# Alternating two heads' attention products between the halves of the matmul array

## The chip, the cores and the metric

The kernel runs on one core of a Trainium2 chip. The metric is the device time of one execution in microseconds (us). [...]

## The reference

The program is a small network of two blocks of two layers each. The change touches only the second block, where a layer is a mixer and a feed-forward part. Layer 0's mixer has, beside a gated part, neighbourhood attention with 8 heads of 64 over 256 tokens, whose keys are the 256 tokens (with a bias and a window) and 256 context tokens; the context stream attends to itself (256 keys). Layer 1's mixer has attention with 16 query heads of 64 and 4 heads of keys and values, over the same 512 keys. What is computed for a head, with q divided by the square root of 64:

```python
s = jnp.einsum('bqhgd,bkhd->bhgqk', qg, k).astype(jnp.float32) * (dh ** -0.5)
p = jax.nn.softmax(s, axis=-1).astype(v.dtype)
return jnp.einsum('bhgqk,bkhd->bqhgd', p, v)
```

## The kernel before

All of it is in float32. A product whose inputs were split into a high and a low part (`float32r`) is three matmuls that add up in PSUM (`mm3`, lines 355 to 357: high by high, high by low, low by high). A product of plain float32 is one matmul that shows as two records in the trace.

`attend_pair` does the attention of two heads whose q and k lie in partitions 0 to 63 and 64 to 127. It is called 16 times: in `even_mixer` for each of four chunks once for the context (`nk` = 256 keys) and once for the tokens (`nk` = 512, with a bias), in `odd_mixer` for each of eight chunks (`nk` = 512, with a scale). Before the change it goes head by head. For a head, and for each of two tiles `t` of 128 queries, it does

- the scores: three matmuls of 64 rows by 128 columns (lines 355 to 357) into a PSUM bank `sc`, of which there are two;
- `softmax`: the row maximum on DVE (line 1239, or 1236 with the bias added), its negative (1243, 1246), the exponential with the row sum on ACT (1244, 1247), the reciprocal and the scaling on DVE (1249, 1250);
- four (or two) transposes of the probabilities on PE (line 1268) into the one PSUM bank `pt`, and their copies to SBUF on ACT (line 1271) into tiles `pT`, of which there are four; a tile holds two blocks of 128 keys for both query tiles.

When a head's two tiles are done, the value products follow (line 1273): one matmul for each block `j` of 128 keys, 128 rows by 64 columns, into the head's half of the bank `po`. Then `split` (lines 1039, 1040) writes the result of both heads.

The instructions are not run in the order in which they are written: a scheduler orders each engine's queue ahead of time, instruction by instruction, from priorities that follow the written order, and from when it expects operands and buffers to be ready. So other matmuls, called fill below, stand between those of the attention: in `even_mixer` the projections of the next chunk and the gate (`project`, `gelu2`), in `odd_mixer` the projections of later queries (`query`) and the output projection (`out_products`). They are the matmuls into `acc`.

Of the kernel before, what the change touches and what calls it, by code (L numbers as in the profile page):

```python
# [13 lines left out]
PSUM = bass.MemoryType.PSUM  # L14
# [27 lines left out]
def block_list():  # L42
    """The weight blocks in the order in which they are used: (weight, layer, first chunk of 128 rows,
    number of chunks, first column, columns)."""
    out = []
# [98 lines left out]
def host_arrays(inp):  # L144
    """The inputs laid out for the chip, and constants that depend on shapes alone."""
    import numpy as np

    f = {k: np.asarray(v) for k, v in inp.items()}
    a = {}
# [130 lines left out]
class Net:  # L280
# [23 lines left out]

# [1 line left out]
    def con(self, pool, i):  # L306
# [11 lines left out]

# [1 line left out]
    def load(self):  # L320
# [16 lines left out]
    def weights(self, n=1):  # L337
        """The next n blocks: (hi, lo) by chunk of rows."""
        i = self.nuse
        self.nuse += n  # L340
        while self.nload < min(self.nuse + self.ahead, len(BLOCKS)):
            self.load()
        out = []
        for j in range(i, i + n):
            hi, lo = self.loaded.pop(j)
            out += [(hi[:, k], lo[:, k]) for k in range(BLOCKS[j][3])]
        return out
# [11 lines left out]
    def gemm(self, w, m, xs, cols, n, ps=None):  # L359
        """[128 columns m of the block, n tokens] in PSUM; xs: (hi, lo) by chunk."""  # L360
        if ps is None:
            ps = self.psum("acc")[:, :n]
        m = slice(128 * m, 128 * m + 128)
        for k, (wk, xk) in enumerate(zip(w, xs, strict=True)):
            self.mm3(ps, [t[:, m] for t in wk], [t[:, cols] for t in xk], k == 0, k == len(w) - 1)
        return ps

    def gemm_nat(self, w, xs, t, n, ps=None, m=0, first=True, last=True):
        """[128 tokens t, n columns of the block] in PSUM."""
        if ps is None:  # L370
            ps = self.psum("acc")[:, :n]
        m = slice(m, m + n)
        for k, (wk, xk) in enumerate(zip(w, xs, strict=True)):
            self.mm3(ps, [x[:, t] for x in xk], [x[:, m] for x in wk], first and k == 0, last and k == len(w) - 1)
        return ps

# [1 line left out]
    def rsqrt(self, src, shape, mul, add, name, pool=None):  # L378
        """1/sqrt(src * mul + add) on a small tile; RS^2 times its argument too if it goes to a pool of its own.
        A guess from the bits, a step of Newton with constants for the least error (under 7e-4), then one of third  # L380
        order (under 1e-9); the argument's factor RS^2 makes up for the factors that the steps leave out."""
        nc = self.nc
# [18 lines left out]
    def rsqrt1(self, a, b, name):  # L401
        """1/sqrt(a + b + 1024 eps), [128, 1], for columns RS^2 a and RS^2 b of sums over 1024 features, as rsqrt."""
        nc = self.nc
# [11 lines left out]
    def sumsq_add(self, ss, tmp_pool, src, first, n):  # L415
        """ss (+)= src^2, [128, n]."""
        nc = self.nc
# [7 lines left out]
    def rstd_row(self, pool, ss, tiles, width, mul, name, eps=EPS, extra=False):  # L425
        """[128, n] with 1/sqrt(mean + eps) of each token in each partition, from sums over chunks; and by
        token: the same and mean + eps, with a column for tokens 0 to 31 four times if extra."""
        nc = self.nc
# [19 lines left out]

# [1 line left out]
    def ada_prepare(self):  # L450
# [12 lines left out]
    def ada_steps(self):  # L463
        """Generator: the conditioning by groups of four units of 512 columns, each unit in rows of its own; a
        step is half of the columns for one chunk of the contraction."""
        nc = self.nc
# [42 lines left out]

# [1 line left out]
    def first_pre(self, c, g, sums=True):  # L511
        """The scaled, not yet normalized operand of chunk c of h, and its part of the sum of squares."""
        nc = self.nc
# [47 lines left out]
    def first_mixer(self, l, mp, fp):  # L561
# [17 lines left out]

        # queries and keys, not divided by the norm of h: its square joins eps in their own norms  # L580
        n_a = 42 if l == 0 else 40
# [39 lines left out]

        # recurrent branch: parameters
        bh = mp.tile([128, 8], F32, name="bh")
# [39 lines left out]

        # recurrent branch, and the first tile of queries
        xc, gts = [], []
# [62 lines left out]

        # output projection, recurrent half last
        oc = slice(0, T) if l + 1 < DEPTH else slice(META, T)  # L730
# [16 lines left out]
    def first_attend(self, mp, l, i, qk, vn, aq, nlam, sub, mh, ml):  # L747
        """Generator: the attention of a tile of queries, a step for each unit of heads and one for the rest."""
        nc = self.nc
# [81 lines left out]
    def gelu2(self, pool, out, x, n):  # L831
        """out = 2 * gelu(x), with the tanh form."""
        nc = self.nc
# [6 lines left out]
    def softplus(self, pool, L):  # L840
        """log(1 + exp(-L)) = max(-L, 0) + 2 atanh(z / (2 + z)), z = exp(-|L|), on [128, 4]."""
        nc = self.nc
# [30 lines left out]
    def first_ffn(self, l, gp, other):  # L873
        """other: steps of work that can be done in between."""
        nc = self.nc
# [51 lines left out]
    def ffn_whole(self, up):  # L927
        """Feed-forward of 256 tokens with the whole result in PSUM: [tile][half], natural."""
        y = [[self.psum("y") for _ in range(2)] for _ in range(2)]
# [25 lines left out]

# [1 line left out]
    def derive(self, l):  # L957
        """Gains of the norms before the branches, joined with the conditioning, times sqrt(1024)."""
        nc = self.nc
# [21 lines left out]
    def pair(self, n):  # L981
        """Room for both parts of a chunk of n tokens."""
        op = lambda: self.chunk(self.c2s, "op", OP_BUFS, F32R)
# [9 lines left out]
    def prepare_steps(self, l, i, s, xs, col, scratch, room, tag):  # L993
        """Generator: the operands of branch i (0: mixer, 1: feed-forward) for stream s, from column col on."""
        nc = self.nc
# [25 lines left out]
    def post(self, t, y, B, scratch, room):  # L1021
        """h += gate * gain * norm(y) for the tokens of tile t; y: two halves."""
        nc = self.nc
# [56 lines left out]
    def second_start(self):  # L1080
        """Room of the second block, and its second stream, which doesn't need the first block."""
        self.der = []
# [8 lines left out]
    def out_products(self, mp, y, half, mix, toks):  # L1091
        """One half of the products of the output projection; the second one on call, by tile of tokens."""
        nc = self.nc
# [135 lines left out]
    def softmax(self, pool, ps, nk, bias, scale):  # L1229
        """Rows of softmax(scale * ps + bias), [128, nk]; scale is None or a column."""  # L1230
        nc = self.nc
# [21 lines left out]
    def attend_pair(self, mp, heads, k0, nk, bias, scale, v, out):  # L1253
        """Two heads of 64: their results transposed, [128, 256], split into out.
        heads: (both parts of q of 256 tokens, of k, column of v) with q and k at rows 0 and 64."""
        nc = self.nc
        po = self.psum("po")[:, :256]
        for i, (q, k, vc) in enumerate(heads):
            r = slice(64 * i, 64 * i + 64)
            nj = nk // 128  # L1260
            pT = [self.chunk(mp, "pT", 4) for _ in range(nj // 2)]
            for t in range(2):
                ps = self.psum("sc")
                self.mm3(ps[:, :nk], [x[r, 128 * t:128 * t + 128] for x in q], [x[r, k0:k0 + nk] for x in k], True, True)
                p = self.softmax(mp, ps[:, :nk], nk, bias and bias(i, t), scale and scale(i, t))
                pt = self.psum("pt")
                for j in range(nj):
                    nc.tensor.transpose(pt[:, 128 * j:128 * j + 128], p[:, 128 * j:128 * j + 128], self.idt)  # L1268
                for jj in range(nj // 2):
                    dst = pT[jj].rearrange("p (j q) -> p j q", j=2)[:, :, 128 * t:128 * t + 128]  # L1270
                    nc.scalar.activation(dst, pt[:, 256 * jj:256 * jj + 256].rearrange("p (j q) -> p j q", j=2), AF.Copy)
            for j in range(nj):
                nc.tensor.matmul(po[r], v[k0 // 128 + j][:, vc:vc + 64], pT[j // 2][:, 256 * (j % 2):256 * (j % 2) + 256],  # L1273
                                 start=j == 0, stop=j == nj - 1, tile_position=(0, 64 * i))
        self.split(out, slice(0, 256), po)
# [196 lines left out]
```

## Time and profile before

| what | value |
|---|---|
| time, median of 3 runs | 1753.16 us (1750.38 to 1757.98) |
| span of the profiled execution | 1758.4 us |
| PE busy | 1700.8 us, 97% of the span |
| DVE, ACT busy | 1165.5 us (66%), 852.1 us (48%) |
| attention in the even mixer | about 799 to 914 us from the start of the span |
| attention in the odd mixer | about 1426 to 1542 us |

The span runs from the first to the last instruction of one profiled execution; no other time of that execution is shown. Busy time of an engine is the time in which at least one of its instructions runs.

### The profile page before, as it was taken

The numbers are of one execution on the slowest core, as the hardware profiler recorded it, in microseconds if no ns is written. First come the engines' busy times: TensorE is split into PE (matmuls) and PEld (weight loads), VectorE is DVE, ScalarE is ACT, GpSimd is POOL, SyncE is SP. The second block draws the span as 40 slices with busy tenths as digits, with TensorE's granted clock in tenths as the row PEclk, the third lists the DMA queues.
The fourth block names the chain that finished last, engine by engine and source line by source line (L and its number), as shares of the span: only waits on it lengthen the run. The fifth ranks groups of instructions, "written<-read, shape, count | busy, mean of one in ns | idle before, by whom it ended". The sixth has DMA issues, their size and how long they took to land.

```text
span 1758.4 us, 27995 instructions
## 1 busy us (share of the span) xinstructions
PE 1700.8 (97%) x10720; PEld 1419.9 (81%) x10720; DVE 1165.5 (66%) x2611; ACT 852.1 (48%) x1615; POOL 69.2 (4%) x142
## 2 busy tenths in 40 slices
PE   8999999999889999999999999999999899979998
PEld 7869999998559999996667777777888776569997
DVE  7678776676757766744557655464666866577777
ACT  5565444455636444534455543233233745565554
POOL 0000000000110000000100111010000000000000
PEclk9999999999999999999999999999999899989999
DMA  7446555553486666432223455464232321136663
GB/s 265 126 145 204 179 170 178 157 180 121 156 279 215 182 189 185 142 100 72 70 78 112 164 198 179 143 210 138 85 98 87 106 66 37 59 97 184 189 184 116
DMA packets 71797, 256.83 MB, mean 146 GB/s; under 512 B 8512, under 2 KB 8528, under 8 KB 71664
## 3 DMA queue, kind: packets, MB, share of 16 engines
q1 hardware_dynamic: 56624, 202.54, 37.7%
q0 software_dynamic: 14896, 52.51, 8.9%
q8 instruction: 84, 1.38, 0.3%
q14 instruction: 49, 0.40, 0.1%
q10 hardware_dynamic: 144, 0.00, 0.0%
HBM read 253.94 MB, written 1.08 MB: 145 GB/s over the span
## 4 chain that ended last, share of the span: by engine, by line
PE 86%; issue 6%; DVE 3%; DMA 3%; ACT 1%; POOL 0%; DVEq 0%; POOLq 0%; ACTq 0%
PE acc L355 16%; PE acc L356 16%; PE acc L357 15%; PE up L355 6%; PE up L356 6%; PE up L357 6%; PE po L1273 3%; DMA wada<-wada 3%; PE acc L476 2%; PE y L355 2%; PE y L357 2%; PE y L356 2%; PE pt L1268 2%; PE sc L355 1%; DVE wlo L333 1%
## 5 line engine op out<-in xcount | busy, mean ns | idle before, releaser
L332 ACT ACTIVATE whi<-raw 128x1024 fp32r<-128x1024 f32 (+2 forms) x436 | 397.0, 924 | 562.4 <-PE acc L356 254.1
L333 DVE TENSOR_TENSOR wlo<-raw,whi 128x1024 fp32r<-128x1024 f32 (+2 forms) x436 | 457.2, 1057 | 284.7 <-ACT whi L332 278.7
L355 PE MATMUL acc<-hi,whi 128*128 128x272 f32 (+1 forms) x848 | 248.0, 293 | 7.4 <-ACT hi L516 7.4
L357 PE MATMUL acc<-hi,wlo 128*128 128x272 f32 (+1 forms) x848 | 246.3, 290 | 0.8 <-DVE wlo L333 0.8
L356 PE MATMUL acc<-lo,whi 128*128 128x272 f32 (+1 forms) x848 | 246.9, 291 | 0.0
L355 PEld LDWEIGHTS acc<-hi,whi 128*128 128x128 f32 x848 | 161.6, 191 | 13.8 <-ACT hi L516 7.4
L356 PE MATMUL acc<-op,whi 128*128 128x256 f32 (+1 forms) x528 | 165.8, 315 | 0.2 <-DVE op L1018 0.2
L355 PE MATMUL acc<-op,whi 128*128 128x256 f32 (+1 forms) x528 | 164.7, 314 | 0.3 <-ACT qraw L1407 0.3
L357 PE MATMUL acc<-op,wlo 128*128 128x256 f32 (+1 forms) x528 | 164.1, 311 | 0.0
L356 PEld LDWEIGHTS acc<-lo,whi 128*128 128x128 f32 x848 | 161.6, 191 | 2.1 <-issue 0.4
L357 PEld LDWEIGHTS acc<-hi,wlo 128*128 128x128 f32 x848 | 161.9, 191 | 1.2 <-DVE wlo L333 0.8
L355 PE MATMUL acc<-whi,op 128*128 128x512 f32 (+1 forms) x432 | 154.9, 358 | 0.0
L356 PE MATMUL acc<-wlo,op 128*128 128x512 f32 (+1 forms) x432 | 154.1, 357 | 0.0
L355 PE MATMUL up<-op,whi 128*128 128x512 f32 (+1 forms) x384 | 147.0, 384 | 0.2 <-ACT pt L1016 0.2
L356 PE MATMUL up<-op,whi 128*128 128x512 f32 (+1 forms) x384 | 146.1, 381 | 0.0
L357 PE MATMUL up<-op,wlo 128*128 128x512 f32 (+1 forms) x384 | 145.4, 379 | 0.0
L355 PEld LDWEIGHTS acc<-op,whi 128*128 128x128 f32 x528 | 100.9, 192 | 10.0 <-issue 3.0
L356 PEld LDWEIGHTS acc<-op,whi 128*128 128x128 f32 x528 | 101.3, 192 | 8.9 <-issue 3.8
L357 PEld LDWEIGHTS acc<-op,wlo 128*128 128x128 f32 x528 | 101.4, 192 | 6.1 <-issue 1.9
L355 PEld LDWEIGHTS acc<-whi,op 128*128 128x128 f32 x432 | 81.2, 188 | 16.1 <-issue 4.6
L356 PEld LDWEIGHTS acc<-wlo,op 128*128 128x128 f32 x432 | 81.4, 188 | 15.0 <-issue 3.4
L355 PEld LDWEIGHTS up<-op,whi 128*128 128x128 f32 x384 | 73.0, 191 | 20.1 <-issue 5.4
(409 smaller groups left out, 3395.0 us busy)
## 6 DMA issues: line engine op xcount, KB each, us to landing
raw<-wts SPq DMA_DIRECT2D x362, 512.0 KB, 3.6
wada<-wada POOLq DMA_DIRECT2D x93, 512.0 KB, 4.7
raw<-wts SPq DMA_DIRECT2D x8, 384.0 KB, 3.1
B<-brow SPq DMA_DIRECT2D x6, 512.0 KB, 4.0
nb<-nbias POOLq DMA_DIRECT2D x16, 128.0 KB, 2.4
wada<-wada SPq DMA_DIRECT2D x3, 512.0 KB, 4.7
h<-xm SPq DMA_DIRECT2D x4, 272.0 KB, 5.0
gates<-gates SPq DMA_DIRECT2D x2, 512.0 KB
```

The costliest lines, as they stand in the source:

```text
L332: nc.scalar.activation(hi[:, cs], raw[:, cs], AF.Copy)
L333: nc.vector.tensor_tensor(lo[:, cs], raw[:, cs], hi[:, cs].bitcast(F32), op=ALU.subtract)
L355: mm(out, a[0], b[0], start=start, stop=False)
L356: mm(out, a[0], b[1], start=False, stop=False)
L357: mm(out, a[1], b[0], start=False, stop=stop)
L476: nc.tensor.matmul(ps[32 * j:32 * j + 32, 256 * half:256 * half + 256], self.cs[:, k], w[:, j], start=k == 0, stop=k + 1 == KD, tile_posit ...
L1268: nc.tensor.transpose(pt[:, 128 * j:128 * j + 128], p[:, 128 * j:128 * j + 128], self.idt)
L1273: nc.tensor.matmul(po[r], v[k0 // 128 + j][:, vc:vc + 64], pT[j // 2][:, 256 * (j % 2):256 * (j % 2) + 256], start=j == 0, stop=j == nj - ...
```

## The change

For one query tile the scores of both heads are now issued matmul by matmul in turn, head 0 in rows 0 to 63 of the array and head 1 in rows 64 to 127, each into a bank of its own. Then come the softmax, the transposes and the copies of head 0 and of head 1. When both query tiles of both heads are done, the value products are issued in turn, for each block of keys head 0 in columns 0 to 63 and head 1 in columns 64 to 127. The four `pT` tiles of a pair (two with 256 keys) are taken at once. The number of instructions, their shapes and the numbers of buffers are the same. Elsewhere the diff takes out comments alone.

```diff
     def attend_pair(self, mp, heads, k0, nk, bias, scale, v, out):
...
+        nc = self.nc
+        mm = nc.tensor.matmul
+        nj = nk // 128
+        rows = [slice(64 * i, 64 * i + 64) for i in range(2)]
         po = self.psum("po")[:, :256]
-        for i, (q, k, vc) in enumerate(heads):
-            r = slice(64 * i, 64 * i + 64)
-            nj = nk // 128
-            pT = [self.chunk(mp, "pT", 4) for _ in range(nj // 2)]
-            for t in range(2):
-                ps = self.psum("sc")
-                self.mm3(ps[:, :nk], [x[r, 128 * t:128 * t + 128] for x in q], [x[r, k0:k0 + nk] for x in k], True, True)
-                p = self.softmax(mp, ps[:, :nk], nk, bias and bias(i, t), scale and scale(i, t))
+        pT = [[self.chunk(mp, "pT", 4) for _ in range(nj // 2)] for _ in heads]
+        for t in range(2):
+            tok = slice(128 * t, 128 * t + 128)
+            ps = [self.psum("sc")[:, :nk] for _ in heads]
+            for n, (a, b) in enumerate(((0, 0), (0, 1), (1, 0))):
+                for i, (q, k, _) in enumerate(heads):
+                    mm(ps[i], q[a][rows[i], tok], k[b][rows[i], k0:k0 + nk], start=n == 0, stop=n == 2)
+            for i in range(2):
+                p = self.softmax(mp, ps[i], nk, bias and bias(i, t), scale and scale(i, t))
                 pt = self.psum("pt")
                 for j in range(nj):
                     nc.tensor.transpose(pt[:, 128 * j:128 * j + 128], p[:, 128 * j:128 * j + 128], self.idt)
                 for jj in range(nj // 2):
-                    dst = pT[jj].rearrange("p (j q) -> p j q", j=2)[:, :, 128 * t:128 * t + 128]
+                    dst = pT[i][jj].rearrange("p (j q) -> p j q", j=2)[:, :, tok]
                     nc.scalar.activation(dst, pt[:, 256 * jj:256 * jj + 256].rearrange("p (j q) -> p j q", j=2), AF.Copy)
-            for j in range(nj):
-                nc.tensor.matmul(po[r], v[k0 // 128 + j][:, vc:vc + 64], pT[j // 2][:, 256 * (j % 2):256 * (j % 2) + 256],
-                                 start=j == 0, stop=j == nj - 1, tile_position=(0, 64 * i))
+        for j in range(nj):
+            for i, (_, _, vc) in enumerate(heads):
+                mm(po[rows[i]], v[k0 // 128 + j][:, vc:vc + 64], pT[i][j // 2][:, 256 * (j % 2):256 * (j % 2) + 256],
+                   start=j == 0, stop=j == nj - 1, tile_position=(0, 64 * i))
         self.split(out, slice(0, 256), po)
```

## Rows read from the trace of the kernel before

**Rows 1.** The page: span, and the first line on engines.

```profile
span 1758.4 us, 27995 instructions
PE 1700.8 (97%) x10720; PEld 1419.9 (81%) x10720; DVE 1165.5 (66%) x2611; ACT 852.1 (48%) x1615; POOL 69.2 (4%) x142
```

**Rows 2.** Busy time by stretch: even attention, odd attention, what follows.

```profile
core 0: us, PE busy (x) PEld busy (x) DVE busy (x) ACT busy (x) POOL busy (x), PEclk, DMA share, GB/s
799.00:914.00 115.00, 115.00 (x509) 73.55 (x508) 63.56 (x182) 57.10 (x146) 11.88 (x30) 1.00 0.19 58
1426.00:1542.00 116.00, 116.00 (x553) 73.02 (x553) 69.08 (x210) 65.81 (x169) 0.00 (x0) 1.00 0.17 51
```

**Rows 3.** Waits, 1426 to 1542: who for whom, us, times, longest.

```profile
ACT pT L1271 <- PE pt L1268: 25.5, 29, 2.2
PEld po L1273 <- ACT pT L1271: 4.5, 13, 0.4
```

**Rows 4.** The same stretches, instructions on tile sc alone, then on po alone.

```profile
799.00:914.00 115.00, 23.90 (x96) 13.27 (x96) 17.57 (x32) 9.01 (x32) 1.00 0.19 58
1426.00:1542.00 116.00, 31.38 (x96) 14.95 (x96) 22.08 (x32) 27.62 (x64) 1.00 0.17 51
...
799.00:914.00 115.00, 25.00 (x96) 11.49 (x96) 3.40 (x8) 3.07 (x8) 1.00 0.19 58
1426.00:1542.00 116.00, 32.55 (x128) 15.63 (x128) 3.40 (x8) 3.07 (x8) 1.00 0.17 51
```

**Rows 5.** Timeline, PE: first block's scores, conditioning; start us, duration, line, form.

```profile
437.87 0.73 PE L766 MATMUL sc<-kr,qr 64*128 64x272 f32 x4
...
452.92 0.72 PE L766 MATMUL sc<-kr,qr 64*128 64x272 f32 x2
...
462.32 1.07 PE L476 MATMUL acc<-wada,cs 128*32 128x256 f32 x16
```

**Rows 6.** Timeline, PE: scores in the even and the odd mixer.

```profile
804.75 0.51 PE L355 MATMUL sc<-qkv 64*128 64x256 f32 x2
...
1434.02 0.49 PE L355 MATMUL sc<-y,qh 64*128 64x512 f32 x1
1434.44 1.94 PE L1273 MATMUL po<-pT,v 128*64 128x256 f32 x8
...
1436.89 0.50 PE L356 MATMUL sc<-y,qh 64*128 64x512 f32 x1
...
1524.12 0.49 PE L355 MATMUL sc<-y,qh 64*128 64x512 f32 x1
...
1525.71 0.50 PE L355 MATMUL acc<-whi,op 128*128 128x512 f32 x1
...
1528.02 0.50 PE L355 MATMUL sc<-y,qh 64*128 64x512 f32 x1
...
1528.91 0.50 PE L355 MATMUL acc<-whi,op 128*128 128x512 f32 x1
```

**Rows 7.** Timeline, PE: end of a pair in the odd mixer.

```profile
1516.62 0.66 PE L1268 MATMUL pt<-con,p 128*128 128x128 f32 x4
...
1518.09 0.66 PE L1268 MATMUL pt<-con,p 128*128 128x128 f32 x4
...
1519.38 1.08 PE L1273 MATMUL po<-pT,v 128*64 128x256 f32 x4
...
1520.82 1.08 PE L1273 MATMUL po<-pT,v 128*64 128x256 f32 x4
```

**Rows 8.** Groups by line and form, 1426 to 1542: count, busy us, mean ns.

```profile
L1247 ACT ACTIVATE p<-sc,snm,aq 128x512 f32<-128x512 f32 x32 | 24.9, 780 | 3.4 <-DVE snm L1246 3.3
...
L1271 ACT ACTIVATE pT<-pt 128x256 f32<-128x256 f32 x64 | 21.0, 380 | 25.5 <-PE pt L1268 25.5
...
L1250 DVE TENSOR_SCALAR p<-p,sr 128x512 f32<-128x512 f32 x32 | 15.5, 483 | 0.4
...
L1247 ACT ACTIVATION_READ_ACCUMULATOR p<-sc,snm,aq 128x1 f32 x32 | 6.5, 204 | 0.0
```

## The prediction

> **What bounds the kernel now.** I read the page first: PE is busy for 97% of the span, and a matmul's end is modelled there, so that alone doesn't say that PE sets the pace [rows 1]. The busy time by stretch comes next. In both stretches of attention PE is busy for all of 115 and of 116 us, while DVE has 55 to 60% and ACT 50 to 57%, at a granted clock of 1.00 [rows 2]. Then the waits decide who waits for whom: in the odd stretch ACT's copies stood idle 25.5 us for transposes from PE, while the weight loads of the value products waited only 4.5 us in total for ACT's copies, never over 0.4 us at a time [rows 3]. So in both stretches PE's queue is the bound, and the softmax runs ahead of it. Fill from other parts still stands between the attention's matmuls in the last pair of the odd stretch, at 1525.71 and 1528.91 [rows 6], so there is work that can move up. A microsecond taken off PE here is a microsecond off the end.
>
> How much is there to take? In the two stretches, instructions on the score banks keep PE busy for 23.9 and 31.4 us, those on the value bank for 25.0 and 32.6 us [rows 4]. Half of the 112.8 us, 56 us, is the ceiling for anything that lets two heads run side by side.
>
> **Can halves of the array run side by side?** The trace of before has it in other places. The first block's scores for two heads' halves of rows take 0.73 us as four records, and those of one half alone take 0.72 us as two records: the second half is free [rows 5]. For columns, the conditioning's products go to four groups of 32 columns: sixteen records of 256 columns take 1.07 us [rows 5], while four records of 256 columns in one head's half of `po` take 1.08 us [rows 7]. And even the scores of this very function do it by chance: two first matmuls together take 0.51 us, where one takes 0.50 (at 804.75, one of ten such places in the two stretches, each of a single matmul) [rows 6]. So I cost a matmul that goes beside one of the other half at nothing.
>
> **Prices.** Three score matmuls of 512 keys that stand alone take 0.89 us (1528.02 to 1528.91); six in a row take 1.59 us (1524.12 to 1525.71), so three more in the same run cost 0.70 us [rows 6]. For 256 keys I take half, an estimate. Value products: eight records, four products, take 1.94 us [rows 6], four records, two products, 1.08 us [rows 7]; a product costs 0.43 us.
>
> **If every product finds its partner.** There are 64 groups of three score matmuls, 48 of them with 512 keys: each stretch has 96 score matmuls [rows 4], 16 groups of the even one being narrow. The change makes 32 rounds of them, 24 wide and 8 narrow. A wide round saves 0.70 to 0.89 us, a narrow one half: 16.8 to 21.4 and 2.8 to 3.6 us. Of value products a wide pair has eight, a narrow one four, and half are hidden: 12 pairs at 4 x 0.43 = 1.72 us, or 1.94 where a whole run goes, and 4 at 0.86 to 1.08 us: 24.0 to 27.6 us. Together 44 to 53 us. That is one end.
>
> **What the order does to it.** The written order alternates, but the queue's order comes from readiness, instruction by instruction: the score group of 1434.02 is cut after its first matmul by eight value records and transposes, and its second comes at 1436.89 [rows 6]. In step with that, look at when partners become ready.
>
> Scores: head 0's bank is free when its exponential has run, head 1's one exponential later, 0.78 + 0.20 = 0.98 us [rows 8]. Head 0's three matmuls need 0.70 us. Unless PE is held up by something else, all three are gone before head 1 may start; they then pair with nothing. Both banks free at the same time is what a run of six, or one that begins to be one, shows. I find ten of those in the two stretches, the run at 1524.12 being one [rows 6], against 32 rounds. I take ten rounds that pair, four narrow and six wide: 4 x 0.35 + 6 x 0.70 = 5.6 us. Today's ten chance overlaps hide some 0.15 us each, and I let them go: 1.5 us. Net 4 us. The ends are -1.5 and 25 us.
>
> Value products: near the end of a pair two sets of transposes follow each other after 1.47 us, and the first product starts 1.29 us after the set that it needs [rows 7]. After the change these two sets are head 0's and head 1's of the second query tile. So head 0's first product starts before head 1's transposes; these (0.66 us) go next, and two copies of 0.38 us must follow [rows 8] before head 1 has its operands. Meanwhile head 0's second and third product run, and from there on both heads have products ready. Of eight, head 0's first stands alone, and the other seven take about five slots: six instead of eight. 2 x 0.43 us x 12 wide pairs = 10.3 us. In a narrow pair one of four: 0.43 x 4 = 1.7 us. Sum 12 us, ends 0 (head 0 always done first) and 27.6. The split into several runs costs nothing new: the last head of a pair is already split in two today, at 1519.38 and 1520.82 [rows 7].
>
> At 804.75 the two that run together stand next to each other in the queue [rows 6]. [...]
>
> **Other edits.** Softmax, transposes and copies keep their number and sizes; no DMA moves with them. The four `pT` go to one pair, so the first copy of the next pair waits for this pair's last value products, and behind it on ACT's queue stand exponentials and the casts of weights. I cost this at nothing: the next pair's transposes come behind these products anyway, and fill covers what is left. Its price without cover is the third rival.
>
> **Sum.** 4 + 12 = 16 us of PE. 1758.4 - 16 = 1742.4 us for an execution like the profiled one, whose span is 0.3% above the median; in the median's terms 1753.16 x 1742.4 / 1758.4 = 1737 us. With 16 us less PE work, ACT stands at 66 of some 108 us in the odd stretch, so it does not become the bound.
>
> **Rivals.**
> - All partners meet. If the scheduler's clock sees PE behind the softmax, as the chip does [rows 3], both heads' operands lie ready and the written order holds. 35 to 53 us: 1700 to 1718 us. Against it stands the cut group of 1434.02. Chance 0.15.
> - The alternation doesn't happen. Every first head is done before the second is ready; only the order of tiles changes. Then it gains or loses up to 9 us by what the scheduler puts elsewhere: 1744 to 1762 us. For it: 0.98 against 0.70 us. Chance 0.27.
> - Slower, by the `pT` tiles. If the next pair's first copies (0.76 us) and the exponential queued behind them (0.98 us) start only after the last value product, and no fill is ready, PE waits 1.7 us at each of 16 boundaries: 28 us, less the 16 us gained, 1765 us. It decides from 1 us of open wait at a boundary on. Against it: PE's fill between pairs, and PE now waits 0.4 us at most [rows 3]. Chance 0.08.
>
> The forecast, some partners meeting, has 0.50 and its own range 1718 to 1744 us. A measurement of this kernel can tell about 0.5%, 9 us, from no change. Faster: 0.15 + 0.50 = 0.65; same 0.27; slower 0.08. The range for 8 in 10 goes from 1712, in the first rival, to 1757, which leaves the slower rival and the top of the second out.
>
> **What would show it.** Right: both stretches shorter by 16 us together, by more in values than in scores; value records of both halves starting together in part, runs of sixteen records in some 3 us instead of two runs of eight at 1.94; most score groups still three matmuls of one head. Full alternation: score groups of six in 0.89 us throughout, and sixteen value records in 1.94. [...]

## The result and the profile after

| kernel | median | range of its runs |
|---|---|---|
| before | 1755.36 us | 1750.38 to 1757.98 (4 runs) |
| changed | 1726.58 us | 1726.08 to 1729.71 (4 runs) |

The ratio is 0.9839, with a 95% interval of 0.9819 to 0.9860: about 28 us faster (25 to 32). The forecast was 1737 us in a range of 1712 to 1757, faster with a chance of 0.65. The sign and the range held; the gain was 28 us where 16 were forecast.

The page of the changed kernel, span and first line on engines; [rows 1] are those of before. PE stands for TensorE's matmuls and PEld for its weight loads, listed apart; DVE is VectorE, ACT ScalarE, POOL GpSimd.

```profile
span 1725.0 us, 27991 instructions
...
PE 1669.8 (97%) x10720; PEld 1403.9 (81%) x10720; DVE 1163.6 (67%) x2611; ACT 851.0 (49%) x1615; POOL 69.8 (4%) x142
```

PE has the same number of records and 31 us less busy time, at the same share of a shorter span. DVE and ACT do what they did.

Busy time by stretch in the changed kernel, from the first score to the last value product of the even and of the odd attention. Columns as in [rows 2].

```profile
796.00:900.00 104.00, 103.59 (x505) 66.91 (x505) 62.15 (x181) 56.92 (x147) 12.14 (x28) 1.00 0.22 64
1412.00:1509.00 97.00, 96.97 (x546) 63.86 (x545) 67.95 (x208) 64.96 (x168) 0.00 (x0) 1.00 0.20 58
```

PE is still busy throughout at a granted clock of 1.00; ACT has risen to 67% of the odd stretch (64.96 of 97) and is not the bound. From the first score to the last value product the stretches were 113.0 and 113.9 us long in the profiled execution before (799.6 to 912.6, 1426.0 to 1539.9) and are 103.7 and 97.0 now (796.1 to 899.8, 1412.0 to 1508.9): 26.2 us less. The two spans differ by 33.4 us, more than the medians, because the profiled execution of before was one of the longer ones; the other 7 us are spread over the first 800 us (3.6), the time between the stretches (1.2) and the end (2.4).

Waits in the odd stretch of the changed kernel; [rows 3] are those of before.

```profile
ACT pT L1275 <- PE pt L1272: 15.3, 23, 1.2
...
PEld po L1278 <- ACT pT L1275: 3.5, 10, 0.4
```

Nothing has turned round: ACT's copies still wait for PE, and the weight loads of the value products wait 0.4 us at most for the copies.

Busy time with instructions on `po` alone, even and odd stretch of the changed kernel; [rows 4] are those of before.

```profile
790.00:915.00 125.00, 17.24 (x96) 7.60 (x96) 3.39 (x8) 3.04 (x8) 1.00 0.26 79
1400.00:1526.00 126.00, 20.70 (x128) 9.89 (x128) 3.39 (x8) 3.06 (x8) 0.98 0.19 58
```

The same view with instructions on `sc`, even stretch.

```profile
790.00:915.00 125.00, 22.19 (x96) 11.08 (x96) 17.14 (x32) 8.60 (x32) 1.00 0.26 79
```

The value products took 57.55 us of PE before and take 37.94 now. The scores of the even stretch went only from 23.90 to 22.19.

Busy times overlap at their ends, so for a balance I give each matmul the time from its start to the start of the next one on PE, and add these up by kind over both stretches ("PE time" from here on):

| PE time, us | before | changed | difference | forecast |
|---|---|---|---|---|
| scores | 50.6 | 45.8 | -4.8 | -4 |
| value products | 54.6 | 35.7 | -18.9 | -12 |
| transposes | 27.8 | 26.1 | -1.7 | 0 |
| fill | 93.9 | 93.1 | -0.8 | 0 |

What the queue does shows in the timeline of PE over a pair of the odd mixer (start us, duration, line, form, count).

```profile
1411.96 0.73 PE L1267 MATMUL sc<-y,qh 64*128 64x512 f32 x4
1412.53 0.39 PE L1267 MATMUL sc<-y,ql 64*128 64x512 f32 x2
1412.86 0.39 PE L355 MATMUL acc<-op,whi 128*128 128x256 f32 x1
...
1419.12 0.72 PE L1267 MATMUL sc<-y,qh 64*128 64x512 f32 x2
1419.68 0.39 PE L1267 MATMUL sc<-y,ql 64*128 64x512 f32 x1
1420.00 0.66 PE L1272 MATMUL pt<-con,p 128*128 128x128 f32 x4
...
1421.59 0.65 PE L1278 MATMUL po<-pT,v 128*64 128x256 f32 x2
1422.17 0.66 PE L1272 MATMUL pt<-con,p 128*128 128x128 f32 x4
...
1423.87 1.94 PE L1278 MATMUL po<-pT,v 128*64 128x256 f32 x14
1425.74 0.73 PE L1267 MATMUL sc<-y,qh 64*128 64x512 f32 x4
```

Six scores at 1411.96 take 0.90 us to the next matmul, three at 1419.12 take 0.88: where two heads' scores meet, the second head is free, but this round of three met nobody. Of the value products exactly one (two records) runs alone at 1421.59; head 1's transposes come at 1422.17; the other seven products (fourteen records) then take 1.94 us, the time that eight records took in [rows 6]. It is so in all twelve wide pairs; in the four narrow ones it is one alone and three in two slots. A slot is the time of one product, or of two side by side.

### The profile page after: what moved, and what is told of

It reads as the page before. It is cut to its first block, busy times and chain, and to the rows that moved or that the text cites. A ratio compares the mean times of both kernels' runs of the same rounds, so it can differ in the third digit from the quotient of the medians.

```text
span 1725.0 us, 27991 instructions
## 1 busy us (share of the span) xinstructions
PE 1669.8 (97%) x10720; PEld 1403.9 (81%) x10720; DVE 1163.6 (67%) x2611; ACT 851.0 (49%) x1615; POOL 69.8 (4%) x142
## 4 chain that ended last, share of the span: by engine, by line
PE 80%; issue 12%; DMA 3%; DVE 3%; ACT 1%; POOL 1%; DVEq 0%; POOLq 0%; SPq 0%; ACTq 0%
PE acc L355 15%; PE acc L356 15%; PE acc L357 15%; PE up L355 6%; PE up L356 6%; PE up L357 6%; DMA wada<-wada 3%; PE sc L1267 3%; PE y L355 2%; PE y L357 2%; PE y L356 2%; PE po L1278 2%; PE acc L476 2%; PE pt L1272 2%; DVE wlo L333 1%
```

## The experiments

All diffs are against the changed kernel. A "round" is the scores of both heads for one query tile. Ratios are to the kernel before, run on the same chip; PE time is as defined above.

| kernel | median us | ratio, 95% interval | PE time scores | PE time values |
|---|---|---|---|---|
| before | see below | 1 | 50.6 | 54.6 |
| changed | 1726.58 | 0.9839 (0.9819 to 0.9860) | 45.8 | 35.7 |
| e1, only values in turn | 1734.03 | 0.9881 (0.9867 to 0.9896) | 48.9 | 35.7 |
| e2, only scores in turn | 1740.38 | 0.9925 (0.9913 to 0.9937) | 45.2 | 45.5 |
| e3, neither in turn | 1743.32 | 0.9933 (0.9917 to 0.9950) | 45.9 | 46.5 |
| e9, old tile order, values in turn | 1729.36 | 0.9869 (0.9851 to 0.9887) | 49.2 | 35.7 |
| e4, head 1 first | 1719.62 | 0.9799 (0.9786 to 0.9812) | 45.5 | 27.7 |
| e10, two by two | 1718.37 | 0.9801 (0.9787 to 0.9814) | 45.4 | 28.3 |
| e7, two value banks | 1736.35 | 0.9890 (0.9878 to 0.9903) | 43.0 | 43.1 |
| e5, scores tied | 1753.63 | 0.9984 (0.9973 to 0.9995) | 48.5 | 44.5 |
| e11, tied and head 1 first | 1732.22 | 0.9869 (0.9855 to 0.9884) | 45.5 | 28.9 |
| e8, scores behind | 1802.71 | 1.0281 (1.0264 to 1.0299) | 66.5 | 53.1 |
| e6, behind and head 1 first | 1784.37 | 1.0178 (1.0158 to 1.0198) | 70.6 | 36.3 |

In e5, e6, e8 and e11 the PE time holds waits of PE as well. The medians of before, on the chip of the run, are 1753.74 us for e1 to e4, 1754.31 for e6 and e8 to e10, and 1755.75 for e5, e7 and e11.

### Which of the parts gives the time: e1, e2, e3, e9

e1: the scores of a round are written head by head again, the value products stay in turn.

```diff
-            for n, (a, b) in enumerate(((0, 0), (0, 1), (1, 0))):
-                for i, (q, k, _) in enumerate(heads):
+            for i, (q, k, _) in enumerate(heads):
+                for n, (a, b) in enumerate(((0, 0), (0, 1), (1, 0))):
                     mm(ps[i], q[a][rows[i], tok], k[b][rows[i], k0:k0 + nk], start=n == 0, stop=n == 2)
```

> The new loops, but scores head by head (three of head 0, then three of head 1); only the value products alternate. Theory (matmul time saved in the two stretches of attention comes off the end one for one; values save 19 us, scores 5 us): 22 to 24 us under the kernel before, ratio 0.987. Rival (the gain is from the new order of tiles, not from halves side by side): like the changed kernel, ratio 0.984.

e2: the scores stay in turn, the value products are written head by head.

```diff
-        for j in range(nj):
-            for i, (_, _, vc) in enumerate(heads):
+        for i, (_, _, vc) in enumerate(heads):
+            for j in range(nj):
                 mm(po[rows[i]], v[k0 // 128 + j][:, vc:vc + 64], pT[i][j // 2][:, 256 * (j % 2):256 * (j % 2) + 256],
```

> The new loops, scores in turn, but value products head by head (all of head 0, then all of head 1). Theory: 5 us from scores and a few from value products of the two heads that meet by chance, 5 to 10 us under the kernel before, ratio 0.994 to 0.997. Rival (new order of tiles): ratio 0.984.

e3: both edits, so that only the order of tiles and the place of the value products at the end of the pair are new.

> The new loops, with scores and value products both head by head. Theory: within 5 us of the kernel before, ratio 0.997 to 1.003. Rival (new order of tiles): 20 us or more under it, ratio 0.988 or less.

e3 was to be within 5 us of before and was some 11 us faster (0.9933; 1743.32 against 1753.74 us). Nothing in it is written in turn, yet its value products take 46.5 us of PE time instead of 54.6 and its scores 45.9 instead of 50.6. PE's timeline shows how (e3, a pair of the odd mixer).

```profile
1430.15 0.65 PE L1278 MATMUL po<-pT,v 128*64 128x256 f32 x2
1430.73 0.66 PE L1272 MATMUL pt<-con,p 128*128 128x128 f32 x4
1431.31 2.48 PE L1278 MATMUL po<-pT,v 128*64 128x256 f32 x14
...
1475.16 0.75 PE L1267 MATMUL sc<-y,qh 64*128 64x512 f32 x4
1475.74 0.41 PE L1267 MATMUL sc<-y,ql 64*128 64x512 f32 x2
1476.08 0.50 PE L357 MATMUL acc<-whi,op 128*128 128x512 f32 x1
```

Fourteen records in 2.48 us are neither the four slots of the changed kernel nor what the written order would give if matmuls started strictly in it: three products of head 0, the last one at best beside head 1's first, and three more of head 1, six slots, some 2.8 us by the steps below. Their starts form two chains, with a first step of 0.27 us and then steps of 0.216 us: one of six records from 1431.312 to 1432.442, three products of head 0, and one of eight from 1431.855 on, four of head 1. Written order puts all six of head 0 first; the first of head 1 starts when three of them have not started. Five of the twelve wide pairs look like this one; the others are cut in other ways. In the six scores at 1475.16, written three and three, the second head's matmuls start 10 ns after those of the first, one beside the other. So if the queue holds them as they are written, PE itself brought heads together that stand one behind the other, as I read it once the operands of both were ready. What makes both ready is the new order of tiles or the new place of the value products; e3 has both and does not part them.

e1 and e2 then price the parts on one chip. e1 came in some 20 us under before where 22 to 24 were expected, e2 some 13 us where 5 to 10 were. Values in turn on top of e3: 1743.32 to 1734.03, 9.3 us, with 10.8 us less PE time in values and 3.0 more in scores. Scores in turn on top of e3: 1743.32 to 1740.38, 2.9 us, with intervals that overlap. On top of e1, where the values are in turn already, scores in turn give the changed kernel: 0.9881 to 0.9839, some 7 us, with intervals that do not overlap, and 3.1 us less PE time in scores. So what the turn of the scores is worth depends on what else stands in the queue.

e9: the old order of tiles and the old scores, and only the value products moved to the end of the pair and written in turn.

```diff
-        for t in range(2):
-            tok = slice(128 * t, 128 * t + 128)
-            ps = [self.psum("sc")[:, :nk] for _ in heads]
...
+        for i, (q, k, _) in enumerate(heads):
+            for t in range(2):
+                tok = slice(128 * t, 128 * t + 128)
+                ps = self.psum("sc")[:, :nk]
```

> Head by head through both query tiles, as before, but the value products of the pair at its end and in turn. Theory (scores gain from the new order of tiles, which puts the two heads' score groups next to each other, not from being written in turn): values as in the changed kernel, scores as before the change, 50 us of TensorE for them instead of 46; 20 to 24 us under the kernel before, ratio 0.987. Rival (the new order of tiles gives nothing by itself): as the run that alternates values alone, 0.988, with scores at 49 us in both.

Its value time is that of the changed kernel, 35.7 us, and its score time stays near that of before, 49.2. So the value gain needs neither the new order of tiles nor the scores in turn; products at the end of the pair and in turn are enough. The score gain is not pinned. The theory had 50 us for scores here and the rival 49 in both runs, and 49.2 and 48.9 are nearer to the rival; the two ratios, 0.9869 and 0.9881, have intervals that overlap. The changed kernel, e2 and e3 have 45 to 46 us, e1 and e9 49, and e1 and e3 write their scores in the same way.

### What holds back the value products: e4, e10, e7

In the changed kernel head 0's first product runs before head 1's operands are there, and head 0's second and third did not go ahead of head 1's first. If the queue keeps the written order of products into one bank, then writing head 1 first must bring all eight together.

e4:

```diff
         for j in range(nj):
-            for i, (_, _, vc) in enumerate(heads):
+            for i, (_, _, vc) in reversed(list(enumerate(heads))):
```

> The changed kernel, but in each block of keys the value product of head 1 is written before that of head 0. Theory (products into one bank keep the written order, so today head 0's first one goes alone, 0.58 us in each of 16 pairs, ahead of head 1's transposes): all products of a pair in one run, sixteen records in 1.94 us, 9 us less than the changed kernel, ratio to the kernel before 0.979. Rival (the lone product only fills time in which TensorE would wait for head 1's copies): as the changed kernel, 0.984.

It came in at 0.9799. Busy time with instructions on `po`, even and odd stretch of e4:

```profile
790.00:915.00 125.00, 12.13 (x96) 6.19 (x96) 3.40 (x8) 3.07 (x8) 1.00 0.27 80
1400.00:1526.00 126.00, 15.58 (x128) 8.49 (x128) 3.38 (x8) 3.08 (x8) 0.95 0.20 59
```

and a pair in its timeline of PE:

```profile
1417.44 0.63 PE L1272 MATMUL pt<-con,p 128*128 128x128 f32 x4
...
1419.02 1.95 PE L1278 MATMUL po<-pT,v 128*64 128x256 f32 x16
1420.90 0.73 PE L1267 MATMUL sc<-y,qh 64*128 64x512 f32 x3
```

All sixteen records take 1.95 us, four slots, and the lone product is gone: 27.71 us against 37.94.

e10 keeps head 1 first but writes two products of head 1, then two of head 0, and so on. If matmuls start strictly in the order of the queue, this takes five slots in a wide pair; if PE looks past a waiting matmul, four.

```diff
-        for j in range(nj):
-            for i, (_, _, vc) in enumerate(heads):
+        for jj in range(0, nj, 2):
+            for i, j in ((1, jj), (1, jj + 1), (0, jj), (0, jj + 1)):
+                vc = heads[i][2]
```

> As the run with head 1 first, but the value products stand in the queue two of head 1, two of head 0, two of head 1, two of head 0. Theory (TensorE starts a matmul for the free half ahead of some that wait for the busy half): a pair's run stays at 1.94 us for sixteen records, ratio 0.980. Rival (matmuls start strictly in the order of the queue): five slots of 0.43 us instead of four, 2.4 us for a run, 5 to 7 us more than with heads in turn, ratio 0.983 to 0.984.

The ratio is 0.9801 and the run takes 2.00 us. PE's timeline of e10:

```profile
1418.14 2.00 PE L1279 MATMUL po<-pT,v 128*64 128x256 f32 x16
```

Two windows at the start of that run, instructions on `po` alone; the number in brackets counts the records that run in a window.

```profile
1418.14:1418.15 0.01, 0.01 (x1) 0.01 (x1) 0.00 (x0) 0.00 (x0) 1.00 0.00 0
1418.15:1418.16 0.01, 0.01 (x2) 0.01 (x2) 0.00 (x0) 0.00 (x0) 1.00 0.00 0
```

The second record starts at 1418.156, 13 ns after the first. The next record of the same head starts 0.27 us after the first, so the early one must be head 0's, in front of which, by the written order, three records of head 1 still waited. So neither in e10 nor in e3 did matmuls start strictly in the order of the queue, if the queue holds the products of a bank as they are written. The rival would be that the scheduler put e10's products back in turn. Against it, the starts are not those of e4: in all 16 pairs the second record starts 13 or 14 ns after the first in e10, 6 or 7 ns in e4, and late in the wide pairs of e10 the distance grows to some 57 ns. The queue itself is not shown, and the records don't name their half, so which record is whose rests on the written order and the steps of 0.216 us.

e7 gives head 1's products a bank of their own, `st`; the results are then split in two steps, which adds 16 instructions each to ACT and DVE.

```diff
-        po = self.psum("po")[:, :256]
+        pos = [self.psum(n)[:, :256] for n in ("po", "st")]
...
-                mm(po[rows[i]], v[k0 // 128 + j][:, vc:vc + 64], pT[i][j // 2][:, 256 * (j % 2):256 * (j % 2) + 256],
+                mm(pos[i][rows[i]], v[k0 // 128 + j][:, vc:vc + 64], pT[i][j // 2][:, 256 * (j % 2):256 * (j % 2) + 256],
...
-        self.split(out, slice(0, 256), po)
+        for r, po in zip(rows, pos):
+            self.split([o[r] for o in out], slice(0, 256), po[r])
```

> The changed kernel, with head 1's value products in a PSUM bank of their own (the one of the small sums); the result is then split in two parts of 64 partitions, 16 more instructions each on ACT and DVE. Theory (one bank keeps the written order): with two banks the queue follows readiness, two of head 0's products go before head 1's transposes in narrow pairs, and values take 2 to 5 us more of TensorE; ratio 0.985 to 0.988. Rival (the order comes from readiness alone): values and time as in the changed kernel, 0.984.

0.9890: values now take 43.1 us of PE time, 7.4 more than in the changed kernel, and the gain shrinks by some 9 us (0.9890 against 0.9839). Both are beyond what was expected, and not quite in the way that was expected: in the narrow pairs all eight records make one run, behind head 1's transposes, with head 0 ahead in it. Timeline of PE in e7:

```profile
1424.68 0.65 PE L1278 MATMUL po<-pT,v 128*64 128x256 f32 x2
1425.26 0.66 PE L1272 MATMUL pt<-con,p 128*128 128x128 f32 x4
1425.85 0.86 PE L1278 MATMUL po<-pT,v 128*64 128x256 f32 x3
1426.39 0.43 PE L1278 MATMUL st<-pT,v 128*64 128x256 f32 x1
1426.54 0.38 PE L1278 MATMUL po<-pT,v 128*64 128x256 f32 x1
```

Here the tile names the head. Head 0 (`po`) is 0.54 us ahead when head 1 (`st`) begins, as in e3. With a bank for each head the products no longer keep the written turn, and head 0 runs ahead as readiness would have it; with one bank they keep it. The added split is part of that, so the time alone does not price the bank; that the order of the records does not hang on the split is likely, but not shown.

### Can the scores be made to meet: e5, e11, e8, e6

e5 chains the six scores of a round in the queue, one after the other, head 1 first.

```diff
+            last = None
             for n, (a, b) in enumerate(((0, 0), (0, 1), (1, 0))):
-                for i, (q, k, _) in enumerate(heads):
-                    mm(ps[i], q[a][rows[i], tok], k[b][rows[i], k0:k0 + nk], start=n == 0, stop=n == 2)
+                for i in (1, 0):
+                    q, k, _ = heads[i]
+                    with self.tc.issue_after(last) if last else nullcontext():
+                        m = mm(ps[i], q[a][rows[i], tok], k[b][rows[i], k0:k0 + nk], start=n == 0, stop=n == 2)
+                    last = m.ins
```

> The changed kernel, with the six score matmuls of a round in one fixed order, head 1 first, each queued behind the one before it; so head 0 can't run ahead alone, and nothing waits for transposes. Theory (TensorE's time counts; a round pairs at the price of one lone matmul): scores 4 to 8 us less of TensorE than in the changed kernel, ratio 0.980 to 0.982. Rival (any later score is waited for): idle gaps of TensorE, ratio 0.986 or more.

It lost nearly all that the change had gained: 0.9984. Busy time by stretch in e5:

```profile
790.00:915.00 125.00, 122.78 (x569) 79.34 (x568) 64.62 (x184) 62.08 (x154) 12.63 (x31) 0.96 0.25 78
1412.00:1530.00 118.00, 108.04 (x565) 67.32 (x564) 71.66 (x210) 66.82 (x171) 0.00 (x0) 0.93 0.17 50
```

PE idles 10 us of the 118 around the odd stretch, and the granted clock falls to 0.93. In 12 of the 32 rounds one score runs alone and the other five come later. Scores of two heads start within 25 ns of each other at 65 of 96 places (34 in the changed kernel), but the waits cost more than that gives.

e11 is e5 with the value products of head 1 first, e4's edit.

> Both: scores tied as above, and head 1's value product first in each block. Theory: the gains add, ratio 0.976 to 0.978. Rival: as with head 1 first alone, 0.980, or more.

0.9869, so the gains do not add: e4's edit is worth 21 us on top of e5 (1753.63 to 1732.22), more than on the changed kernel, but tying still costs some 12 us against e4 alone (0.9869 against 0.9799).

e8 queues the six scores of a round behind the last transposes of the round before, when both banks are free.

```diff
+            with self.tc.issue_after(self.behind) if self.behind else nullcontext():
                 for n, (a, b) in enumerate(((0, 0), (0, 1), (1, 0))):
...
-                    nc.tensor.transpose(pt[:, 128 * j:128 * j + 128], p[:, 128 * j:128 * j + 128], self.idt)
+                    self.behind = nc.tensor.transpose(pt[:, 128 * j:128 * j + 128], p[:, 128 * j:128 * j + 128], self.idt).ins
```

> The changed kernel, with each round's six score matmuls queued behind the last transpose of the round before, when both score banks are free. Theory (TensorE sets the pace, so pairs that are always complete gain): scores take 36 to 40 us of TensorE instead of 46, 6 to 9 us less than the changed kernel, ratio 0.979. Rival (scores that start later make TensorE wait for the softmax): idle gaps of TensorE in the stretches, ratio 0.984 or more.

It is slower than before, 1.0281. Busy time by stretch in e8:

```profile
796.00:910.00 114.00, 98.72 (x460) 64.04 (x460) 57.24 (x164) 51.87 (x130) 10.26 (x26) 0.87 0.20 60
1440.00:1550.00 110.00, 84.78 (x400) 52.11 (x399) 49.36 (x160) 47.10 (x121) 0.00 (x0) 0.77 0.13 41
```

Two of the waits of e8 from 1440 to 1550:

```profile
PEld pt L1273 <- ACT p L1247: 17.9, 5, 3.9
...
PE pt L1273 <- ACT p L1247: 9.6, 3, 3.2
```

With the scores held back, the softmax no longer runs ahead of PE: PE waits for exponentials, up to 3.9 us at a time, and the granted clock falls to 0.77, with PE busy 84.78 of 110 us. The bound of the stretch has changed.

e6 is e8 with head 1 first in the value products.

> Both edits: scores queued behind the transposes, and head 1's value product first in each block. Theory: the two gains add up, ratio 0.975. Rival (later scores are waited for): as with head 1 first alone, 0.980, or more.

1.0178: 18 us better than e8, still slower than before.

## Why the prediction was right, and where its size was off

**PE is the bound, and its time comes off the end.** Right. 26.2 us less PE time in the table above, stretches shorter by 26.2, some 28 us by the ratio. In e1, e2, e3 and e9 the sum of PE time is 22.0, 15.5, 13.3 and 24.5 us under before, and the median 19.7, 13.4, 10.4 and 25.0 us.

**A partner in the other half costs nothing.** Right. Six scores take 0.90 us where three take 0.88; fourteen value records in four slots take 1.94 us like eight in [rows 6].

**Scores, 4 us.** It came to 4.8, but that the two are so near is in part luck. The forecast had ten rounds pairing in full, and let today's chance overlaps go. In the changed kernel only five rounds pair in full, three narrow and two wide, 2.5 us by the prediction's prices; the rest comes with 13 rounds in which one or two matmuls meet. In all it has 34 of 96 places where two scores start within 25 ns, ten before. What brings them about is open: e3 has 34 as well without any turn in the written scores, while taking the turn out of the changed kernel (e1) leaves 26. Nor do the places alone set the time: e1 with 26 and e9 with nine have 48.9 and 49.2 us.

**Values, 12 us.** This term was mis-sized: 18.9 us. The walk let head 0's second and third product run while head 1's transposes and copies went, so that six slots of eight were left. They did not: one product ran alone, and the others then ran in turn, five slots of eight in all, and three of four in a narrow pair as forecast. The forecast saves 2 x 12 + 4 = 28 slots, the changed kernel 3 x 12 + 4 = 40. A slot saved is worth 18.9 / 40 = 0.47 us of PE time, where the prediction had 0.43 from the step within a run. Twelve more slots at 0.47 make 5.7 us, and 0.04 us on 28 slots 1.2: together the 6.9 us that were missing. What failed is the step "meanwhile, head 0's second and third product run". That the queue keeps the turn because both heads share a bank is supported by e7, where head 0 does run ahead, and by e4, where the turn holds from the other side; it is not shown beyond doubt, as e7 adds the split too.

**The rest.** Transposes and fill gave another 2.5 us, which the prediction had at nothing; I have no experiment on that.

**Other edits at nothing.** Right: the `pT` tiles bring no wait, as the waits of the odd stretch show.

**The rivals.** The alternation happens. All partners meeting was nearer for values than I thought: e4 gets there by one edit, 1719.62 us, with the scores still mostly apart. The slower rival, PE waiting between pairs, did not come in this kernel. e8 shows the price when the softmax's lead is lost: 48 us over before (1802.71 against 1754.31).

**A strict order of starts**, the rival in e10, is shown by no run. By e3 and e10, if the queue holds a bank's products as written, PE started the other half's matmul ahead of three records that waited, 0.54 us after the run began in e3 and 13 ns in e10. Yet not all partners met in the changed kernel, and the 44 to 53 us for that did not come. Head 1's operands were not there when the lone product ran, as its transposes came only 0.58 us later.

## What to carry to other kernels

Where two heads can share the array, count slots from when the operands of each come, and write first the head whose operands come last: here that one edit took the gain from 28 to some 35 us (0.9799, or 0.9801 as in e10; these beat both kernels). Let the scheduler order the rest: edges that force partners together made PE wait, and cost some 12 us (e11 against e4) to 76 us (e8 against the changed kernel).

## What was not expected of the hardware

- If the queue holds the products of a bank as they are written, PE started a matmul of the other half ahead of matmuls of the busy half: 0.54 us after the run began in e3, with three records waiting in front, and after 13 ns in e10. Loops that make both heads ready were worth some 11 us with nothing written in turn (e3).
- Plain float32 products of two halves paired record by record: sixteen records in 1.95 us in e4, eight in 1.94 in [rows 6].
- A slot costs 0.43 us inside a run, but 0.49 us of PE time on average over all of them, in three orders: 54.6 / 112 before, 35.7 / 72 in the changed kernel, 27.7 / 56 in e4. The rest falls at the ends of runs: two records that stand alone take 0.58 us to the next matmul (1421.59 to 1422.17 in the changed kernel). Why is open; no run here isolates it.
- In e5 and e8, where PE waits, the granted clock of the odd stretch is lower: 0.93 with PE busy 108 of 118 us (e5), 0.77 with 85 of 110 (e8), where the changed kernel has 1.00 with 97 of 97.
